# Hybrid mixer block on one core: projections with the hi and lo columns of x in one 512-column matmul per weight tile

## The chip, the cores and the metric

The kernel runs on one core of one Trainium2 chip. The metric is the device time of one execution in microseconds (us). The kernel before takes 1879.42 us, the median of three runs (1879.31 to 1880.51).

## The reference

One decoder layer on x of 256 tokens by 2048 channels, all in fp32. `w_in` projects the normalized input to the columns of three token mixers (RG-LRU, gated DeltaNet, RWKV-7) and of three merge gates; the mixers' outputs are projected, gated and summed, and a SwiGLU feed-forward part follows.

```python
h = rms_norm(x, norm_mix_pre)
p = h @ w_in                    # 2048 x 15664: columns of all mixers, then of the gates
lru_x, lru_g, qkv, z, beta_raw, alpha_raw, rw, gate_raw = split_cols(p, IN_SIZES)
y_a = rglru_branch(lru_x, lru_g, ...)
y_b = gated_deltanet_branch(qkv, z, beta_raw, alpha_raw, ...)
y_c = rwkv7_branch(rw, ...)
gates = sigmoid(gate_raw).reshape(B, S, 3, D)
mixed = sum_b gates[:, :, b] * (y_b @ w_branch[b])
x = x + rms_norm(mixed @ w_out, norm_mix_post)
x = x + rms_norm((silu(h2 @ w_gate) * (h2 @ w_up)) @ w_down, norm_ffn_post)   # h2 = rms_norm(x, norm_ffn_pre)
```

## The kernel before

Every large product is made from split operands. An fp32 value v is split into hi, v rounded to the format fp32r, and lo, v - hi; a product is then hi*hi + hi*lo + lo*hi, three fp32r matmuls that add up in the same PSUM bank. The input x is split once: `acts` (line 887) makes the tiles `xh` and `xl`, [128, 16, 256] each (16 k-tiles of 128 channels, 256 tokens), and `feed` (line 901) fills them, on ScalarE and on VectorE. The weights are split as they stream in: `weights` (line 190) loads 1 MB at a time into one of three `raw` tiles over SyncE's queue, ScalarE casts 1024 columns of it to `wh` (line 214), VectorE subtracts and gives `wl` (line 216), and there are three tiles of each.

Two helpers consume weights. `block_a` has tokens on the output partitions and streams 512 weight columns per matmul (lines 262 to 264); it makes the merge gates, the branch products, w_out and the feed-forward part. `block_b` (lines 228 to 246) has channels on the output partitions: the weight tile of 128x128 is the stationary operand and the 256 tokens are streamed, three matmuls for each k and each of two column tiles (lines 241 to 243), all into one PSUM bank [128, 2, 256]. It makes the mixers' projections: w_lo (256 columns), w_lo2 (128 columns) and 36 blocks of 256 columns of w_in. The tag `mm` of these banks has three buffers, which `block_a` uses too (two at a time).

When a bank is full, a sink empties it. `direct` (line 962) has VectorE multiply the bank with the tokens' norm factors `rbc` straight into a slab (`scaled`, line 339); `kept` (line 939, by `put_dram`, line 343) does the same into a stage tile, applies an activation on ScalarE and stores the tile in DRAM, from where `get` loads it later. The two lo blocks go by a ScalarE copy (`raw_slab`, line 948) and are scaled later, in SBUF.

The loop over q (lines 996 to 1011) runs four quarters; each has three rwkv blocks, three DeltaNet blocks and a kept z, and an LRU block and a kept gate, then the rest of the mixer chains, and some gate blocks (`fill`) as other work for TensorE. The mixers invert small triangular matrices (`inverse64`, line 369): 16x16 diagonal blocks go to DRAM and come back spread over all partitions (tile `B`, lines 381 to 384), 1 MB in an rwkv quarter and 512 KB in a DeltaNet pair. The branch products follow, then w_out, the norm, and the feed-forward part, which calls `acts` again for its own input; at the end the norm weights `n4` reuse the tag of `xl` and the output tile `od` that of `xh`.

The program's text sets dependencies and priorities, not the order. A planner simulates the engines in time and writes each engine's list from that; on the chip every engine works through its list in order.

Of the kernel before, what the change touches and what calls it, by code (L numbers as in the profile page):

```python
# [8 lines left out]
F32 = mybir.dt.float32  # L9
F32R = mybir.dt.float32r  # L10
# [4 lines left out]
P = 128  # L15
T = 256
# [62 lines left out]
def lay_out(inp):  # L79
# [43 lines left out]
    for g, key in enumerate(("lru_w_a", "lru_w_x")):  # L123
# [10 lines left out]
        "n2": f["norm_mix_post"], "n4": f["norm_ffn_post"], "w_in": blocks(w_in, 256), "w_mix": blocks(w[:, OFF_GATE:], 512),  # L134
# [6 lines left out]
class Builder:  # L141
# [86 lines left out]
    def block_b(self, wp, pp, src, xh, xl, kts, sink, width=256):  # L228

        for _ in self.block_b_steps(wp, pp, src, xh, xl, kts, sink, width):  # L230
            pass

    def block_b_steps(self, wp, pp, src, xh, xl, kts, sink, width=256):
        nc = self.nc
        ps = pp.tile([P, 2, 256], F32, name=self.uid("mm"), tag="mm", bufs=self.mm_bufs)
        nct = width // P
        for k, h, l in self.weights(wp, src, kts, width):
            for c in range(nct):
                hs, ls = h[:, c * P:(c + 1) * P], l[:, c * P:(c + 1) * P]
                o = ps[:, c]  # L240
                nc.tensor.matmul(o, hs, xh[:, k], start=(k == 0 and c == 0), stop=False, skip_group_check=True)  # L241
                nc.tensor.matmul(o, hs, xl[:, k], start=False, stop=False, skip_group_check=True)  # L242
                nc.tensor.matmul(o, ls, xh[:, k], start=False, stop=(k == kts - 1), skip_group_check=True)  # L243
            yield k
        with self.tc.high_priority(self.ahead_evac):
            sink(ps[:, :nct])
# [92 lines left out]
    def scaled(self, out, ps):  # L339

        self.nc.vector.tensor_tensor(out, ps, self.rbc.unsqueeze(1).to_broadcast([P, ps.shape[1], T]), ALU.mult)

    def put_dram(self, func):

        nc = self.nc
        d = self.dp.tile([P, 512], F32, name=self.uid("keep"))

        def sink(ps):
            t = self.sp.tile([P, 512], F32, name=self.uid("stage"), tag="stage", bufs=self.stage_bufs)
            self.scaled(t.rearrange("p (c t) -> p c t", c=2), ps)  # L350
            if func != AF.Copy:
                nc.scalar.activation(t, t, func)
            nc.scalar.dma_start(d, t)
        return sink, d
# [517 lines left out]
def build(tc, aps, out):  # L872
# [14 lines left out]
    def acts(s):  # L887
        return (xp.tile([P, KD, T], F32R, name=f"{s}h", tag="xh"), xp.tile([P, KD, T], F32R, name=f"{s}l", tag="xl"))
# [6 lines left out]
    xh, xl = acts("x")  # L895
# [40 lines left out]
    def cols(o, sink):  # L936
        b.block_b(wp, pp, w_in[o], xh, xl, KD, sink)

    def kept(o, func=AF.Copy):
        sink, d = b.put_dram(func)  # L940
        cols(o, sink)
        return d
# [5 lines left out]
    def raw_slab(t):  # L948
        return lambda ps: nc.scalar.copy(t[:, 0:ps.shape[1], 1:257], ps)

    b.block_b(wp, pp, aps["w_lo"][0], xh, xl, KD, raw_slab(lo))
# [3 lines left out]
    b.block_b(wp, pp, aps["w_lo2"][0], xh, xl, KD, raw_slab(lo2), width=128)  # L955
    b.scaled(lo[:, :, 1:257], lo[:, :, 1:257])
    b.scaled(lo2[:, 0:1, 1:257], lo2[:, 0:1, 1:257])
# [4 lines left out]
    def direct(o, lead):  # L962

        t = b.slab(lead)
        cols(o, lambda ps: b.scaled(t[:, :, lead:lead + T], ps))
        return t
# [10 lines left out]

    def stage(s):
        return sp.tile([P, 512], F32, name=b.uid(s), tag="stage", bufs=b.stage_bufs)
# [120 lines left out]
    xh, xl = acts("h")  # L1100
# [59 lines left out]
    n4 = full(xp, "n4", aps["n4"], tag="xl")  # L1160
    od = xp.tile([P, 2, D], F32, name="od", tag="xh")
# [38 lines left out]
```

## Time and profile before

| | before |
|---|---|
| median of 3 runs | 1879.42 us |
| profiled execution | 1879.03 us |
| its span, first to last instruction | 1877.3 us |
| TensorE matmuls busy | 1839.9 us, 98% |
| weight loads busy | 1591.6 us, 85% |
| VectorE busy | 1114.8 us, 59% |
| ScalarE busy | 850.5 us, 45% |
| mean granted TensorE clock | 0.988 of full speed |

Matmuls are pipelined: the profile lists each with a duration that overlaps the next one's, so their busy time adds up to a full engine, and what one costs in a row of them is the distance between starts. In the rows, PE is TensorE's matmuls, PEld its weight loads, DVE VectorE, ACT ScalarE, POOL GpSimd and SP SyncE; L241 is line 241; out<-in names the tiles. PEclk is the granted clock, 1.00 for 2.4 GHz. Some matmul records are missing from the trace; a row with x2 or more merges neighbours.

### The profile page before, as it was taken

Reading aid. Unit: us, or ns where it says so; the run is one execution under the profiler, and the core shown is the slowest. Engines: PE = TensorE matmul, PEld = TensorE weight load, DVE = VectorE, ACT = ScalarE, POOL = GpSimd, SP = SyncE. Lnnn points to the kernel's source line nnn. Section 1 sums busy time; section 2 is a strip of 40 time slices with the busy share of each in tenths; the row PEclk is TensorE's granted clock in tenths of the full one; section 3 lists DMA queues with packets and bytes.
Section 4 is the critical chain, followed back from the end, with each engine's and each line's share of the span. In section 5 each row is a group of like instructions: output and inputs, shape, how many; then the busy total and the mean of one; then the engine's idle time right before and its main releaser. Section 6 shows DMA issues by size and latency. Waiting matters only on the chain.

```text
span 1877.3 us, 27855 instructions
## 1 busy us (share of the span) xinstructions
PE 1839.9 (98%) x11516; PEld 1591.6 (85%) x11516; DVE 1114.8 (59%) x1622; ACT 850.5 (45%) x1055; POOL 82.6 (4%) x150
## 2 busy tenths in 40 slices
PE   9999999999999999899999999999999999999997
PEld 9999997999798988677888887888888888888886
DVE  6768667666776577656655556445545444444444
ACT  7445355434543465334444445444444444443442
POOL 0011010200120012000000000000000000000000
PEclk9999999999999999899999999999999999999999
DMA  7565445644565355648655556555555555555553
GB/s 263 183 183 200 141 152 189 169 162 153 178 168 175 134 183 174 202 164 310 209 194 183 195 186 234 194 196 184 194 187 191 191 181 199 204 200 188 194 200 114
DMA packets 61647, 352.06 MB, mean 188 GB/s; under 512 B 9040, under 2 KB 10832, under 8 KB 22480
## 3 DMA queue, kind: packets, MB, share of 16 engines
q1 hardware_dynamic: 50256, 327.18, 50.4%
q10 hardware_dynamic: 6752, 14.31, 2.1%
q0 software_dynamic: 4512, 8.79, 1.9%
q8 instruction: 90, 1.47, 0.3%
q14 instruction: 37, 0.30, 0.0%
HBM read 336.22 MB, written 14.02 MB: 187 GB/s over the span
## 4 chain that ended last, share of the span: by engine, by line
PE 53%; issue 38%; DMA 4%; DVE 3%; ACT 2%; POOL 1%; ACTq 0%; DVEq 0%; POOLq 0%; SPq 0%
PE mm L264 8%; PE mm L263 8%; PE mm L262 8%; PE mm L243 7%; PE mm L242 7%; PE mm L241 7%; DMA raw<-in_w_in_dram 2%; DVE wl L216 1%; DMA B<-dblk 1%; ACT wh L214 1%; PE psa L592 1%; PE pr L585 1%; PE pr L596 1%; PE px L562 0%; PE pst L602 0%
## 5 line engine op out<-in xcount | busy, mean ns | idle before, releaser
L216 DVE TENSOR_TENSOR wl<-raw,wh 128x1024 fp32r<-128x1024 f32 x590 | 720.9, 1223 | 616.8 <-ACT wh L214 614.6
L214 ACT CAST wh<-raw 128x1024 fp32r<-128x1024 f32 x590 | 620.1, 1052 | 856.9 <-PE mm L264 594.8
L241 PE MATMUL mm<-xh,wh 128*128 128x256 f32 x1200 | 344.4, 287 | 5.3 <-ACT wh L214 5.3
L243 PE MATMUL mm<-xh,wl 128*128 128x256 f32 x1200 | 344.9, 288 | 2.1 <-DVE wl L216 1.1
L242 PE MATMUL mm<-xl,wh 128*128 128x256 f32 x1200 | 345.0, 288 | 1.1 <-DVE xl L909 1.0
L263 PE MATMUL mm<-wl,hh 128*128 128x512 f32 x704 | 275.1, 391 | 0.5 <-DVE wl L216 0.5
L264 PE MATMUL mm<-wh,hl 128*128 128x512 f32 x704 | 274.8, 390 | 0.0
L262 PE MATMUL mm<-wh,hh 128*128 128x512 f32 x704 | 250.7, 392 | 2.0 <-DVE rstd L296 1.5
L241 PEld LDWEIGHTS mm<-xh,wh 128*128 128x128 f32 x1200 | 232.2, 194 | 7.5 <-ACT wh L214 6.0
L243 PEld LDWEIGHTS mm<-xh,wl 128*128 128x128 f32 x1200 | 231.9, 193 | 3.9 <-DVE wl L216 1.7
L242 PEld LDWEIGHTS mm<-xl,wh 128*128 128x128 f32 x1200 | 232.1, 193 | 2.4 <-DVE xl L909 1.5
L262 PEld LDWEIGHTS mm<-wh,hh 128*128 128x128 f32 x704 | 132.3, 188 | 29.4 <-ACT hh L311 2.5
L263 PEld LDWEIGHTS mm<-wl,hh 128*128 128x128 f32 x704 | 132.7, 189 | 27.8 <-DVE wl L216 0.7
L264 PEld LDWEIGHTS mm<-wh,hl 128*128 128x128 f32 x704 | 132.6, 188 | 27.5
L263 PE MATMUL mm<-wl,xh 128*128 128x512 f32 x384 | 151.0, 393 | 1.2 <-DVE wl L216 1.1
L264 PE MATMUL mm<-wh,xl 128*128 128x512 f32 x384 | 150.2, 391 | 0.0
L262 PE MATMUL mm<-wh,xh 128*128 128x512 f32 x384 | 139.5, 392 | 0.0
L263 PE MATMUL mm<-wl,ah 128*128 128x512 f32 x352 | 137.0, 389 | 0.0
L264 PE MATMUL mm<-wh,al 128*128 128x512 f32 x352 | 136.9, 389 | 0.0
L262 PE MATMUL mm<-wh,ah 128*128 128x512 f32 x352 | 123.5, 389 | 0.0
L297 POOL TENSOR_TENSOR rstd<-rstd,mhalf 128x8 f32<-128x8 f32 (+3 forms) x23 | 29.7, 1295 | 1453.7 <-DVE rstd L296 1453.7
L263 PEld LDWEIGHTS mm<-wl,xh 128*128 128x128 f32 x384 | 72.1, 188 | 17.8 <-DVE wl L216 2.5
(294 smaller groups left out, 2023.8 us busy)
## 6 DMA issues: line engine op xcount, KB each, us to landing
raw<-in_w_in_dram SPq DMA_DIRECT2D x72, 1024.0 KB, 4.9
raw<-in_w_mix_dram SPq DMA_DIRECT2D x48, 1024.0 KB, 4.9
raw<-in_w_gate_dram SPq DMA_DIRECT2D x44, 1024.0 KB, 4.9
raw<-in_w_up_dram SPq DMA_DIRECT2D x44, 1024.0 KB, 4.8
raw<-in_w_down_dram SPq DMA_DIRECT2D x44, 1024.0 KB, 4.9
raw<-in_w_branch_dram SPq DMA_DIRECT2D x24, 1024.0 KB, 4.9
raw<-in_w_out_dram SPq DMA_DIRECT2D x16, 1024.0 KB, 4.8
keep<-stage ACTq DMA_DIRECT2D x24, 256.0 KB, 5.2
```

The source lines that it names most:

```text
L214: nc.scalar.copy(wh[:, :n], s)
L216: nc.vector.tensor_tensor(wl[:, :n], s, wh[:, :n].bitcast(F32), ALU.subtract)
L241: nc.tensor.matmul(o, hs, xh[:, k], start=(k == 0 and c == 0), stop=False, skip_group_check=True)
L242: nc.tensor.matmul(o, hs, xl[:, k], start=False, stop=False, skip_group_check=True)
L243: nc.tensor.matmul(o, ls, xh[:, k], start=False, stop=(k == kts - 1), skip_group_check=True)
L262: nc.tensor.matmul(ps[t], xh[:, k, ts], h, start=(k == 0), stop=False)
L263: nc.tensor.matmul(ps[t], xh[:, k, ts], l, start=False, stop=False)
L264: return nc.tensor.matmul(ps[t], xl[:, k, ts], h, start=False, stop=(k == kts - 1))
L297: nc.gpsimd.tensor_tensor(r, r, self.mhalf.to_broadcast([P, n]), ALU.pow)
L585: nc.tensor.matmul(pq[bb, us], st[u][:, n, bb], sav[:, n, us], start=not n, stop=True, skip_group_check=True)
L592: nc.tensor.matmul(ps[bb, us], X[bb, 2 * u + p], R[bb, us], start=True, stop=True)
L596: nc.tensor.matmul(pq[ob, us], st[u][:, n, ob], sav[:, n, us], start=not n, stop=True, skip_group_check=True)
```

## The change

`w_in` is laid out in blocks of 128 columns in place of 256. xh and xl become the two halves of one tile x, [128, 16, 2, 256], so that for one k both stand side by side. `block_b` makes two matmuls for each k and column tile in place of three: hi of the weights with both halves of x as one moving operand of 512 columns, which fills a whole bank [128, 2, 256] (first half hi*hi, second half hi*lo), and lo of the weights with hi of x, 256 columns, added to the first half. Each column tile of 128 has a bank of its own. At the eviction `halves` has ScalarE copy the second half to SBUF and VectorE add the first; when both column tiles of a slab are there, `scaled` multiplies them in place. The stage tile of a kept block is taken before its matmuls. In the last part `n4` is loaded into a quarter of the output tile, since both halves of x are now one buffer.

```diff
-        "w_in": blocks(w_in, 256), "w_mix": blocks(w[:, OFF_GATE:], 512),
+        "w_in": blocks(w_in, P), "w_mix": blocks(w[:, OFF_GATE:], 512),
...
-    def block_b_steps(self, wp, pp, src, xh, xl, kts, sink, width=256):
+    def block_b(self, wp, pp, src, xs, kts, sink, width=P):
+
         nc = self.nc
-        ps = pp.tile([P, 2, 256], F32, name=self.uid("mm"), tag="mm", bufs=self.mm_bufs)
         nct = width // P
+        ps = [pp.tile([P, 2, 256], F32, name=self.uid("mm"), tag="mm", bufs=self.mm_bufs) for _ in range(nct)]
         for k, h, l in self.weights(wp, src, kts, width):
             for c in range(nct):
                 hs, ls = h[:, c * P:(c + 1) * P], l[:, c * P:(c + 1) * P]
-                o = ps[:, c]
-                nc.tensor.matmul(o, hs, xh[:, k], start=(k == 0 and c == 0), stop=False, skip_group_check=True)
-                nc.tensor.matmul(o, hs, xl[:, k], start=False, stop=False, skip_group_check=True)
-                nc.tensor.matmul(o, ls, xh[:, k], start=False, stop=(k == kts - 1), skip_group_check=True)
-            yield k
+                nc.tensor.matmul(ps[c], hs, xs[:, k], start=(k == 0), stop=False, skip_group_check=True)
+                nc.tensor.matmul(ps[c][:, 0], ls, xs[:, k, 0], start=False, stop=(k == kts - 1), skip_group_check=True)
         with self.tc.high_priority(self.ahead_evac):
-            sink(ps[:, :nct])
+            for c in range(nct):
+                sink(c, ps[c])
...
-    def scaled(self, out, ps):
-
-        self.nc.vector.tensor_tensor(out, ps, self.rbc.unsqueeze(1).to_broadcast([P, ps.shape[1], T]), ALU.mult)
...
+    def halves(self, out, ps):
+
+        self.nc.scalar.copy(out, ps[:, 1])
+        self.nc.vector.tensor_tensor(out, ps[:, 0], out, ALU.add)
+
+    def scaled(self, t):
+
+        self.nc.vector.tensor_tensor(t, t, self.rbc.unsqueeze(1).to_broadcast([P, t.shape[1], T]), ALU.mult)
...
     def acts(s):
-        return (xp.tile([P, KD, T], F32R, name=f"{s}h", tag="xh"), xp.tile([P, KD, T], F32R, name=f"{s}l", tag="xl"))
+        t = xp.tile([P, KD, 2, T], F32R, name=s, tag="x")
+        return t, t[:, :, 0], t[:, :, 1]
...
-    def cols(o, sink):
-        b.block_b(wp, pp, w_in[o], xh, xl, KD, sink)
-
-    def kept(o, func=AF.Copy):
-        sink, d = b.put_dram(func)
-        cols(o, sink)
+    def cols(o, t):
+
+        for c in range(2):
+            b.block_b(wp, pp, w_in[2 * o + c], xs, KD, lambda _, ps, c=c: b.halves(t[:, c], ps))
+        b.scaled(t)
+
+    def kept(o, func):
+
+        d = b.dp.tile([P, 512], F32, name=b.uid("keep"))
+        t = stage("stage")
+        cols(o, t.rearrange("p (c t) -> p c t", c=2))
+        nc.scalar.activation(t, t, func)
+        nc.scalar.dma_start(d, t)
         return d
...
-    def raw_slab(t):
-        return lambda ps: nc.scalar.copy(t[:, 0:ps.shape[1], 1:257], ps)
-
-    b.block_b(wp, pp, aps["w_lo"][0], xh, xl, KD, raw_slab(lo))
+    b.block_b(wp, pp, aps["w_lo"][0], xs, KD, lambda c, ps: b.halves(lo[:, c, 1:257], ps), width=256)
...
-        cols(o, lambda ps: b.scaled(t[:, :, lead:lead + T], ps))
+        cols(o, t[:, :, lead:lead + T])
...
-    n4 = full(xp, "n4", aps["n4"], tag="xl")
-    od = xp.tile([P, 2, D], F32, name="od", tag="xh")
+    od = xp.tile([P, 4, D], F32, name="od", tag="x")
+    n4 = od[:, 2]
+    nc.scalar.dma_start(n4, aps["n4"].to_broadcast([P, D]))
```

## Rows read from the trace of the kernel before

**Rows 1.** The page, part 1: busy us of each engine, share, instructions.
```profile
PE 1839.9 (98%) x11516; PEld 1591.6 (85%) x11516; DVE 1114.8 (59%) x1622; ACT 850.5 (45%) x1055; POOL 82.6 (4%) x150
```
**Rows 2.** Waits of TensorE: us in total, times, longest us.
```profile
PE mm L241 <- ACT wh L214: 5.3, 2, 3.0
```
**Rows 3.** Waits of VectorE for projection blocks: us in total, times, longest us.
```profile
DVE slab L341 <- PE mm L243: 11.7, 14, 1.6
DVE stage L341 <- PE mm L243: 5.6, 7, 1.2
```
**Rows 4.** Timeline, TensorE, projections: start us, duration us, instruction; first and last of 58.
```profile
53.09 0.28 PE L243 MATMUL mm<-xh,wl 128*128 128x256 f32 x1
...
59.93 0.28 PE L243 MATMUL mm<-xh,wl 128*128 128x256 f32 x1
```
**Rows 5.** Timeline, TensorE, w_down: first and last of 28.
```profile
1699.73 0.39 PE L263 MATMUL mm<-wl,ah 128*128 128x512 f32 x1
...
1705.85 0.39 PE L263 MATMUL mm<-wl,ah 128*128 128x512 f32 x1
```
**Rows 6.** Line 241: count, ns min/median/max, first and last start us.
```profile
L241 PE MATMUL mm<-xh,wh x1200: 277/283/580, 7.4 to 668.5; 128*128 128x256 f32 x172
```
**Rows 7.** Timeline, TensorE, two borders between a projection block and a gate block.
```profile
279.67 0.28 PE L243 MATMUL mm<-xh,wl 128*128 128x256 f32 x1
279.79 0.40 PE L262 MATMUL mm<-wh,xh 128*128 128x512 f32 x1
...
330.05 0.39 PE L264 MATMUL mm<-wh,xl 128*128 128x512 f32 x1
330.28 0.28 PE L241 MATMUL mm<-xh,wh 128*128 128x256 f32 x1
```
**Rows 8.** Timeline, TensorE, around 376 us; in brackets the idle time before.
```profile
376.06 0.39 PE L241 MATMUL mm<-xh,wh 128*128 128x256 f32 x1 [2.27 <-ACT wh L214]
...
377.31 0.58 PE L243 MATMUL mm<-xh,wl 128*128 128x256 f32 x1 [0.69 <-DVE wl L216]
...
378.12 0.41 PE L243 MATMUL mm<-xh,wl 128*128 128x256 f32 x1
...
381.96 0.42 PE L243 MATMUL mm<-xh,wl 128*128 128x256 f32 x1
```
**Rows 9.** Busy us by 25 us: PE, PEld, DVE, ACT, POOL; clock, DMA share, GB/s.
```profile
375.00:400.00 25.00, 23.26 (x295) 22.46 (x296) 20.19 (x66) 9.79 (x11) 0.00 (x0) 0.86 0.56 194
550.00:575.00 25.00, 21.53 (x167) 21.03 (x166) 15.90 (x37) 7.24 (x7) 0.00 (x0) 0.92 0.95 227
575.00:600.00 25.00, 24.02 (x401) 23.13 (x400) 19.19 (x64) 8.14 (x11) 0.00 (x0) 0.95 0.49 173
```
**Rows 10.** DMA issues: queue, count, KB each, median us from issue to landing.
```profile
raw<-in_w_in_dram SPq DMA_DIRECT2D x72, 1024.0 KB, 4.9
B<-dblk POOLq DMA_DIRECT2D x4, 1024.0 KB, 21.5
```
**Rows 11.** The chain of waits in order of time, 350 to 385 us: start us, us.
```profile
357.04 17.82 DMA raw<-in_w_in_dram
```
**Rows 12.** VectorE by line and shape: count, busy us, mean ns; idle before.
```profile
L341 DVE TENSOR_TENSOR slab<-mm,rbc 128x512 f32<-128x512 f32 x28 | 19.2, 686 | 11.7 <-PE mm L243 11.7
...
L859 DVE RECIPROCAL rec<-rec 128x512 f32<-128x512 f32 x4 | 13.4, 3350 | 0.1
...
L608 DVE TENSOR_TENSOR S<-S,pst 128x256 f32<-128x256 f32 x8 | 3.3, 417 | 9.7 <-PE pst L602 9.7
...
L341 DVE TENSOR_TENSOR slab<-slab,rbc 128x512 f32<-128x512 f32 x1 | 0.7, 693 | 0.5 <-ACT rbc L934 0.5
```
**Rows 13.** Line 949, the copies of the two lo blocks: ns min/median/max, first and last start us.
```profile
L949 ACT COPY slab<-mm x2: 367/466/564, 21.2 to 27.7; 128x512 f32<-128x512 f32 x1, 128x256 f32<-128x256 f32 x1
```
**Rows 14.** Busy us by 10 us, columns as in the 25 us stretches.
```profile
250.00:260.00 10.00, 10.00 (x89) 9.60 (x88) 10.00 (x23) 4.53 (x6) 1.30 (x2) 1.00 0.39 133
450.00:460.00 10.00, 10.00 (x90) 9.41 (x89) 10.00 (x24) 3.81 (x6) 0.11 (x1) 1.00 0.44 138
```

More of the change, by code (lines that the diff above doesn't have):

```diff
@@ L133, in lay_out @@
         "x": f["x"][0], "xt": f["x"][0].T.reshape(4, 4, P, T).transpose(0, 2, 1, 3), "par": par, "cst": constants(), "w_lo": blocks(lo[:, :256], 256), "w_lo2": blocks(lo[:, 256:], 128), "lru": lru, "up": up,
-        "n2": f["norm_mix_post"], "n4": f["norm_ffn_post"], "w_in": blocks(w_in, 256), "w_mix": blocks(w[:, OFF_GATE:], 512),
+        "n2": f["norm_mix_post"], "n4": f["norm_ffn_post"], "w_in": blocks(w_in, P), "w_mix": blocks(w[:, OFF_GATE:], 512),
         "w_branch": np.stack([blocks(f["w_branch"][0, i], 512) for i in range(3)]),
@@ L226, in warm_up @@
             self.nc.tensor.matmul(ps, self.rst128[:, 0:P], self.rst128[:, 0:P], start=True, stop=True)
-    def block_b(self, wp, pp, src, xh, xl, kts, sink, width=256):
-        for _ in self.block_b_steps(wp, pp, src, xh, xl, kts, sink, width):
-            pass
-    def block_b_steps(self, wp, pp, src, xh, xl, kts, sink, width=256):
+    def block_b(self, wp, pp, src, xs, kts, sink, width=P):
         nc = self.nc
-        ps = pp.tile([P, 2, 256], F32, name=self.uid("mm"), tag="mm", bufs=self.mm_bufs)
         nct = width // P
+        ps = [pp.tile([P, 2, 256], F32, name=self.uid("mm"), tag="mm", bufs=self.mm_bufs) for _ in range(nct)]
         for k, h, l in self.weights(wp, src, kts, width):
@@ L337, in slab @@
         return t
-    def scaled(self, out, ps):
-        self.nc.vector.tensor_tensor(out, ps, self.rbc.unsqueeze(1).to_broadcast([P, ps.shape[1], T]), ALU.mult)
[L343 to L354, printed above, removed]
+    def halves(self, out, ps):
[3 more added lines that the diff above has]
+        self.nc.vector.tensor_tensor(t, t, self.rbc.unsqueeze(1).to_broadcast([P, t.shape[1], T]), ALU.mult)
     def get(self, d, s):
@@ L892, in build @@
     mp = b.mp = b.pool("mp")
-    xh, xl = acts("x")
+    xs, xh, xl = acts("x")
     xt = [b.u4("x") for _ in range(4)]
@@ L934, in by_token, with stage @@
         nc.scalar.copy(b.rbc, ps[:, 0:T])
-    def cols(o, sink):
-        b.block_b(wp, pp, w_in[o], xh, xl, KD, sink)
-    def kept(o, func=AF.Copy):
-        sink, d = b.put_dram(func)
-        cols(o, sink)
+    def stage(s):
+        return sp.tile([P, 512], F32, name=b.uid(s), tag="stage", bufs=b.stage_bufs)
+    def cols(o, t):
[8 more added lines that the diff above has]
+        nc.scalar.dma_start(d, t)
         return d
@@ L954, in build @@
     input_rms()
-    b.block_b(wp, pp, aps["w_lo2"][0], xh, xl, KD, raw_slab(lo2), width=128)
-    b.scaled(lo[:, :, 1:257], lo[:, :, 1:257])
-    b.scaled(lo2[:, 0:1, 1:257], lo2[:, 0:1, 1:257])
+    b.block_b(wp, pp, aps["w_lo2"][0], xs, KD, lambda c, ps: b.halves(lo2[:, c, 1:257], ps))
+    b.scaled(lo[:, :, 1:257])
+    b.scaled(lo2[:, 0:1, 1:257])
     b.rwkv_lo(lo, lo2)
@@ L976, in gate_block @@
         b.block_a(wp, pp, aps["w_mix"][j], xh, xl, KD, sink)
-    def stage(s):
-        return sp.tile([P, 512], F32, name=b.uid(s), tag="stage", bufs=b.stage_bufs)
     def fill(n):
@@ L1099, in build @@
     x1d = [b.dp.tile([P, D], F32, name=f"x1d{t}") for t in range(2)]
-    xh, xl = acts("h")
+    _, xh, xl = acts("h")
     with tc.high_priority(FIRST):
```

## The prediction

> **What bounds the kernel now.** I read the busy shares first [rows 1]: TensorE's matmuls fill 1839.9 of 1877.3 us. A busy TensorE is not yet a TensorE at its peak, so its list of waits came next [rows 2]: the longest entry is 5.3 us for cast weights, and no eviction of a projection block stands in it. VectorE's own list shows the opposite: for 14 + 7 of the 36 evictions it was VectorE that waited for the matmuls, at most 1.6 us [rows 3]. So in nearly the whole span the time is the sum of what is queued on TensorE. What a matmul costs there is not its listed duration (0.28 us, pipelined), but the distance of starts. In a long row of 256-column matmuls the first and the last of 58 stand at 53.09 and 59.93 us [rows 4]: 6.84/57 = 0.1200 us. In a row of 512-column ones 28 stand between 1699.73 and 1705.85 us [rows 5]: 6.12/27 = 0.2267 us. The difference, 106.7 ns for 256 columns, is the 2.4 GHz level; both leave the same remainder, 120.0 - 106.7 = 13.3 ns and 226.7 - 213.3 = 13.4 ns, whatever the width. At full clock a matmul thus costs its columns plus 13.3 ns.
>
> **The change part by part.** *Fewer, wider matmuls.* A group is one weight tile of 128x128 at one k; there are 1200 of them [rows 6]: 36 blocks of w_in with 2 x 16, w_lo with 32, w_lo2 with 16. Before, a group is three matmuls of 256 columns, 3 x 120.0 = 360.0 ns. After, it is one of 512 and one of 256, 226.7 + 120.0 = 346.7 ns. The columns are the same 768; what goes is one remainder of 13.3 ns and one weight load. 1200 x 13.3 ns = 16.0 us. That needs the two widths to keep their distances when they alternate, which the trace shows only at borders between blocks: a 512 right after a 256 starts 0.12 us behind it, and a 256 right after a 512 0.23 us behind [rows 7], each the distance that belongs to the earlier one's width. I take both as they are, since these rows are the nearest; the bounds are all of the 16.0 us and none.
>
> The Trainium skill (TensorE: Matmul & The Clock Gate, section "Wait — 56ns, not 53.3ns?") gives a fixed cost of about 2.5 ns for a warm matmul, which speaks against the change: an estimate by it is 1200 x 2.5 ns = 3.0 us of gain in place of 16.0. The two distances above show 13.3 ns for this kernel's fp32r matmuls, so the trace does not agree, and the measurement decides.
>
> *Where the saving is lost again.* (a) Half clock. After TensorE had stood still for 2.27 and 0.69 us, starts from 378.12 to 381.96 us lie 3.84/18 = 0.213 us apart for 256 columns [rows 8], which is the 1.2 GHz level; the remainder is gone there, and a group of 768 columns costs 640 ns either way. The granted clock of the stretches around the two stops, 0.86 of 25 us and then 0.92 and 0.95 of 25 us [rows 9], makes 7.0 and 4.0 + 2.5 us at half: 13.5/0.64 = 21 groups without a gain, 0.3 us. (b) Two waits for weights. These stops stand behind the 1 MB transfer that spreads the diagonal blocks (median 21.5 us to landing, against 4.9 for a w_in load [rows 10]); in the chain of waits one w_in load beside it takes 17.82 us [rows 11]. TensorE lives on loaded weights then, for about 22 us or 22/0.36 = 61 groups; it uses them up 61 x 13.3 ns = 0.8 us sooner and waits for the same transfer. Twice, 1.6 us. (c) The start. The first matmuls wait for x; half of w_lo's 32 groups, as I estimate, are fed by arrivals, 16 x 13.3 ns = 0.2 us. That the first matmul of a k now needs lo as well as hi of x costs nothing more, since its successor waited for lo before too.
>
> *Evictions.* Before, 36 blocks each took one multiply of 128x512 on VectorE (0.69 us [rows 12]), the two lo blocks a ScalarE copy each (0.564 and 0.367 us [rows 13]). After, each of 75 column tiles takes a ScalarE copy of 128x256 out of PSUM (0.367 us, the shorter lo copy) and a VectorE add of 128x256 with one operand in PSUM (0.417 us, as the state add [rows 12]); the multiplies stay, now from SBUF (0.693 us, as the one on the first lo slab [rows 12]). Added: on ScalarE 75 x 0.367 - 0.93 = 26.6 us, on VectorE 75 x 0.417 = 31.3 us. The bounds for the time are nothing and all of it, 57.9 us; below nothing it can't go, as it takes no more than the 0.93 us off any engine. I take nothing, because no eviction holds TensorE now and VectorE is busy for 59%, ScalarE for 45% of the span [rows 1]. What covers it are the PSUM banks: three, so a bank must be free two blocks after it is full. That cover was 2 x 96 x 0.120 = 23.0 us and becomes 2 x 16 x 0.3467 = 11.1 us, against 0.37 + 0.42 us of work plus the queues. Behind the copy on ScalarE stand the casts of the next weights and the activations of the mixers; behind the add on VectorE the lo halves of those weights. A finished slab comes 0.37 + 0.42 = 0.8 us later; its readers are mixer chains that TensorE meets between other blocks. If that cover fails, the price is rival 2.
>
> *Edits at nothing.* w_in as blocks of 128 columns still comes in 72 loads of 1 MB, 8 KB per partition, and a 1024-wide cast holds eight groups where it held four pairs, so transfers and casts keep their number; if a load took longer, more waits as in (b) would pay for it. One tile for both halves of x is as large as the two were, and its next user is the norm ahead of the feed-forward part, behind all three branch products. The norm weights for the end now lie in the output tile; their load waits for the same last matmuls as before, and has the first w_down block (44 x 2 x 3 matmuls of 0.2267 us, 60 us) in which to arrive. Taking the stage tile ahead of the matmuls can hold back a gate block for one projection block at most, and TensorE has the projection itself to do meanwhile.
>
> *The sum.* 16.0 - 0.3 - 1.6 - 0.2 = 13.9 us. The profiled execution took 1879.03 us (its span of 1877.3 and 1.7 around it), 0.39 under the median of the three runs, 1879.42. 1879.03 - 13.9 = 1865.1; from the median 1865.5. I say 1865.3 us.
>
> **The rivals.** (1) *A stop more or less.* The order on each engine comes from a planner that simulates time, so changed durations can change the order around the big transfers. A stop as the one at 374 us costs 2.27 + 0.69 us of standing still and 7.0/2 = 3.5 us for the half clock, 6.5 us. One fewer, with the rest of the sum: 1865.1 - 6.5 = 1858.6; one more: 1871.6. For it: that transfer runs in all four quarters and makes a stop in projections in two of them, so it hangs on little. Against: neither the transfer nor its place in the program is touched.
> (2) *Slower, by the bank cover.* VectorE was busy for all of 10 us in stretches where projections run, at 250 and at 450 us [rows 14]. An eviction that crosses two in-order queues and has 11.1 us of cover instead of 23.0 could hold a bank there, TensorE would stop, and the clock fall as in (a). At 6.5 us a stop the sum turns at 13.9/6.5 = 2.1 stops; one in each of three quarters gives 1865.1 + 19.5 = 1884.6. For it: that the same stretch recurs. Against: TensorE did not wait there once (10.00 us busy), and the longest single VectorE instruction, the reciprocal, takes 3.35 us [rows 12].
> (3) *The change doesn't do what it says.* If the 13.3 ns did not belong to each matmul, so that a 512 and a 256 in turn took 360 ns, nothing would be saved: 1879.0. Against it stand the two borders [rows 7]; for it, that they are only two. The skill's 2.5 ns would put the time at an estimated 1876.0, between this case and the forecast.
>
> **How the numbers follow.** The forecast (1861 to 1869) gets 0.66, one stop fewer 0.08, one more but still faster 0.08, no change (rival 3, or two further stops that eat the gain) 0.08, slower by the banks 0.10. A measurement of this kernel can tell about 0.2%, 3.8 us, from no change. That gives 0.82 faster, 0.08 same, 0.10 slower. The range takes in the forecast and both sides of rival 1: from all 16.0 us and one stop fewer, 1879.03 - 16.0 - 6.5 = 1856.5, to one stop more with another 2 us lost, 1873.6; I give 1857 to 1874, with 0.18 left out.
>
> **What would show it.** In the profile after, the two new lines have 1200 matmuls of 512 and 1200 of 256 columns, in turn 0.227 and 0.120 us apart, and TensorE has 10316 matmuls in place of 11516. The last projection group, which began at 668.5 us [rows 6], should begin near 655, and all that follows should keep its length. TensorE's list of waits should not name the add or the copy; if it does, or if stretches of half clock appear beside those near 375 and 570 us, rival 2 is at work. Pairs that take 0.36 us would be rival 3. A shift in the second half, where only the tiles' places change, would make the working wrong.

## The result: 0.95% slower

The changed kernel takes 1897.93 us (median of four runs, 1892.13 to 1900.62) against 1879.37 us for the kernel before on the same chip: a ratio of 1.0095, 95% interval 1.0069 to 1.012. The forecast was 1865.3 us, its range 1857 to 1874. The profiled execution has a span of 1890.4 us, 13.1 more than the 1877.3 of before. It is the fastest of its four, so its trace shows 13.1 of the 18.6 us between the medians; the other three have no trace, and their granted clock was 0.981 to 0.982 in place of 0.986.

The page of after, part 1 (busy us, share, instructions; before: [rows 1]):

```profile
PE 1830.2 (97%) x10316; PEld 1522.0 (81%) x10316; DVE 1137.4 (60%) x1697; ACT 873.6 (46%) x1129; POOL 84.9 (4%) x150
```

TensorE has its 1200 matmuls fewer and is busy for 9.8 us less (1830.17 against 1839.95 to two decimals). It stands still for the rest of the span, 60.2 us where before has 37.3, 22.9 us more: -9.8 + 22.9 = +13.1. That is the whole difference between the two profiled executions, and what has to be explained is the standing still.

Where it lies, by stretches of before (first fence) and after (second); columns: stretch, its us, then busy us of PE, PEld, DVE, ACT, POOL, clock, DMA share, GB/s. The last stretch begins with w_out in both.

```profile
50.00:725.00 675.00, 667.60 (x5759) 616.70 (x5758) 470.39 (x880) 318.49 (x417) 60.10 (x101) 0.99 0.53 170
725.00:850.00 125.00, 116.92 (x892) 94.64 (x891) 78.63 (x165) 52.14 (x76) 12.22 (x20) 0.92 0.56 180
1037.60:1877.30 839.70, 822.52 (x3680) 680.80 (x3678) 423.12 (x418) 362.48 (x423) 7.94 (x10) 0.99 0.54 191
```

```profile
50.00:725.00 675.00, 653.59 (x4624) 547.71 (x4623) 483.80 (x941) 336.36 (x483) 58.74 (x100) 0.99 0.53 169
725.00:850.00 125.00, 107.98 (x866) 88.94 (x865) 80.60 (x171) 54.09 (x79) 14.91 (x23) 0.90 0.51 161
1050.70:1890.40 839.70, 822.51 (x3680) 680.54 (x3678) 423.27 (x418) 362.53 (x423) 8.98 (x10) 0.99 0.55 191
```

The second half keeps its length to the tenth. In the projections TensorE stands still for 675 - 653.6 = 21.4 us (before 7.4), between 725 and 850 us for 17.0 (before 8.1). The last projection group begins at 665.6 us, 2.9 us earlier than before [rows 6] and not the 13 of the forecast. The waits of TensorE in after (us in total, times, longest us; before: [rows 2]) name the engine:

```profile
PE px L396 <- DVE DT L392: 14.5, 1, 14.5
PE mm L237 <- DVE wl L216: 6.6, 4, 3.8
PE mm L236 <- DVE stage L336: 3.5, 1, 3.5
PE mm L236 <- ACT wh L214: 2.8, 2, 1.6
PE mm L256 <- DVE stage L336: 2.3, 2, 1.2
```

L336 is the new add: 3.5 + 2.3 us are matmuls that wait for a PSUM bank. The larger sums are older work on VectorE, the lo halves of weights (L216) and a step of the last quarter's chain (L392). The added instructions are as long as estimated, 0.416 and 0.368 us (columns as in [rows 12]):

```profile
L336 DVE TENSOR_TENSOR slab<-mm,slab 128x256 f32<-128x256 f32 x59 | 24.2, 416 | 0.0
L335 ACT COPY slab<-mm 128x256 f32<-128x256 f32 x59 | 21.3, 368 | 7.2 <-DVE cv L641 6.9 <-PE mm L237 0.3
```

How an add comes to hold TensorE shows in the timeline of after around 267 us (start us, us, engine):

```profile
263.77 0.37 ACT L335 COPY stage<-mm 128x256 f32<-128x256 f32 x1
264.47 0.42 DVE L594 TENSOR_TENSOR S<-S,pst 128x256 f32<-128x256 f32 x1
264.80 0.48 DVE L641 SCALAR_TENSOR_TENSOR cv<-slab,par_t,cv 128x256 f32<-128x256 f32 x1
265.20 1.22 DVE L216 TENSOR_TENSOR wl<-raw,wh 128x1024 fp32r<-128x1024 f32 x1
266.33 0.48 DVE L641 SCALAR_TENSOR_TENSOR cv<-slab,par_t,cv 128x256 f32<-128x256 f32 x1
266.73 0.42 DVE L336 TENSOR_TENSOR stage<-mm,stage 128x256 f32<-128x256 f32 x1
...
267.20 0.80 PE L236 MATMUL mm<-x,wh 128*128 128x512 f32 x1 [3.47 <-DVE stage L336]
```

The copy is done at 264.14, but four instructions stand before the add in VectorE's queue; the add starts at 266.73, 2.6 us later, and TensorE gets the bank at 267.20. In before, TensorE did not stop in this stretch. The 25 us stretches of after, answering to [rows 9] and [rows 14]:

```profile
250.00:275.00 25.00, 21.53 (x141) 18.61 (x140) 18.95 (x42) 11.04 (x19) 1.52 (x4) 0.93 0.27 96
375.00:400.00 25.00, 21.73 (x114) 18.31 (x113) 16.47 (x46) 8.95 (x12) 0.00 (x0) 0.93 0.85 211
450.00:475.00 25.00, 20.60 (x136) 17.20 (x135) 17.74 (x41) 10.50 (x18) 2.10 (x3) 1.00 0.30 102
575.00:600.00 25.00, 19.58 (x102) 16.48 (x102) 14.97 (x43) 7.73 (x10) 0.00 (x0) 0.93 0.84 202
```

Last, the pace. The timeline of after has these two rows of pairs, 512 and 256 columns in turn. In the first there are fifteen 512-column starts from its first line to its last, in the second 58:

```profile
54.71 0.40 PE L236 MATMUL mm<-x,wh 128*128 128x512 f32 x1
54.94 0.28 PE L237 MATMUL mm<-x,wl 128*128 128x256 f32 x1
...
59.65 0.40 PE L236 MATMUL mm<-x,wh 128*128 128x512 f32 x1
...
178.35 0.40 PE L236 MATMUL mm<-x,wh 128*128 128x512 f32 x1
...
198.11 0.39 PE L236 MATMUL mm<-x,wh 128*128 128x512 f32 x1
```

4.94/14 = 0.3529 us a pair in the first and 19.76/57 = 0.3467 in the second; only the second has the pace of the forecast. Over the 1069 pairs of the trace that follow each other directly, 0.33 to 0.37 us apart, the mean is 0.3503 (the expectations of e3 and e8 below say 0.3526, which the trace does not bear out); the 1057 triples of before, counted alike, have 0.3594. That is a saving of 9.1 ns a group, 10.9 us for all 1200 at full clock, close to the 9.8 us by which TensorE's busy time fell.

### The profile page after: what moved, and what is told of

Its sections match the earlier page's. It is cut to its first block, busy times and chain, and to the rows that moved or that the text cites. A ratio compares the mean times of both kernels' runs of the same rounds, so it can differ in the third digit from the quotient of the medians.

```text
span 1890.4 us, 25603 instructions
## 1 busy us (share of the span) xinstructions
PE 1830.2 (97%) x10316; PEld 1522.0 (81%) x10316; DVE 1137.4 (60%) x1697; ACT 873.6 (46%) x1129; POOL 84.9 (4%) x150
## 4 chain that ended last, share of the span: by engine, by line
issue 38%; PE 27%; DMA 2%; DVE 2%; ACT 1%; POOL 0%; DVEq 0%; POOLq 0%; ACTq 0%
PE mm L257 7%; PE mm L258 7%; PE mm L256 7%; PE mm L236 2%; DMA B<-dblk 1%; PE mm L237 1%; DMA raw<-in_w_branch_dram 1%; DVE wl L216 0%; DVE x L1101 0%; PE psa L578 0%; PE pr L571 0%; PE pr L582 0%; PE pst L588 0%; DVE xt L378 0%; PE tp L279 0%
## 5 line engine op out<-in xcount | busy, mean ns | idle before, releaser
L216 DVE TENSOR_TENSOR wl<-raw,wh 128x1024 fp32r<-128x1024 f32 x590 | 720.4, 1223 | 629.8 <-ACT wh L214 628.5
L236 PE MATMUL mm<-x,wh 128*128 128x512 f32 x1200 | 432.0, 402 | 8.0 <-DVE stage L336 3.5
L237 PE MATMUL mm<-x,wl 128*128 128x256 f32 x1200 | 342.9, 286 | 6.7 <-DVE wl L216 6.6
L236 PEld LDWEIGHTS mm<-x,wh 128*128 128x128 f32 x1200 | 227.8, 190 | 61.7 <-DVE stage L336 3.7
L257 PE MATMUL mm<-wl,h 128*128 128x512 f32 x704 | 274.8, 390 | 0.5 <-DVE wl L216 0.5
L258 PE MATMUL mm<-wh,h 128*128 128x512 f32 x704 | 274.8, 390 | 0.0
L256 PE MATMUL mm<-wh,h 128*128 128x512 f32 x704 | 250.8, 391 | 2.0 <-DVE rstd L290 1.5
L237 PEld LDWEIGHTS mm<-x,wl 128*128 128x128 f32 x1200 | 229.4, 191 | 9.9 <-DVE wl L216 8.4
L256 PEld LDWEIGHTS mm<-wh,h 128*128 128x128 f32 x704 | 132.3, 188 | 29.5 <-ACT h L305 2.5
L258 PEld LDWEIGHTS mm<-wh,h 128*128 128x128 f32 x704 | 132.6, 188 | 27.6
L257 PE MATMUL mm<-wl,x 128*128 128x512 f32 x384 | 151.5, 395 | 0.0
L258 PE MATMUL mm<-wh,x 128*128 128x512 f32 x384 | 150.6, 393 | 0.0
L256 PE MATMUL mm<-wh,x 128*128 128x512 f32 x384 | 142.7, 395 | 2.3 <-DVE stage L336 2.3
L256 PEld LDWEIGHTS mm<-wh,x 128*128 128x128 f32 x384 | 72.3, 189 | 18.5 <-DVE stage L336 2.7
L258 PEld LDWEIGHTS mm<-wh,x 128*128 128x128 f32 x384 | 72.5, 189 | 15.3 <-issue 0.7
```

What stands on the lines that cost most here:

```text
L216: nc.vector.tensor_tensor(wl[:, :n], s, wh[:, :n].bitcast(F32), ALU.subtract)
L236: nc.tensor.matmul(ps[c], hs, xs[:, k], start=(k == 0), stop=False, skip_group_check=True)
L237: nc.tensor.matmul(ps[c][:, 0], ls, xs[:, k, 0], start=False, stop=(k == kts - 1), skip_group_check=True)
L256: nc.tensor.matmul(ps[t], xh[:, k, ts], h, start=(k == 0), stop=False)
L257: nc.tensor.matmul(ps[t], xh[:, k, ts], l, start=False, stop=False)
L258: return nc.tensor.matmul(ps[t], xl[:, k, ts], h, start=False, stop=(k == kts - 1))
```

## The experiments

Two theories stood against each other. *Work*: the added copies and adds take time on VectorE and ScalarE that the mixers' chains need. *Order*: the planner, given other durations, puts the instructions of VectorE in another sequence, and TensorE waits behind it. Diffs are against the kernel named in bold; "ratio" is to the kernel before. The first three kernels below (e1 to e3) were planned anew, so each holds another order besides its edit.

### Which part of the change costs

**After**, each column tile evicted by one multiply of the first half (the three lo tiles by one ScalarE copy), and without the multiply of the whole slab:

```
-        self.nc.scalar.copy(out, ps[:, 1])
-        self.nc.vector.tensor_tensor(out, ps[:, 0], out, ALU.add)
...
+            self.nc.vector.tensor_tensor(out, ps[:, 0], self.rbc, ALU.mult)
```

> The changed kernel, but each column tile is emptied by one instruction: VectorE multiplies the first half of the bank by the norm factors straight into its place (the three lo tiles: one ScalarE copy). The second half of the bank, hi of the weights by lo of x, is left out of the result; the matmuls that make it are all there. Theory A (the added ScalarE copies and VectorE adds slow the mixers' chains, and the chains set the time, so the saving on TensorE is lost): without them the saving is kept, 1879 less 5 to 9 us, 1868 to 1876 us. Theory B (the evictions are covered; the planner's other order and the late weight loads cost the time): it stays near the changed kernel, 1890 to 1900 us.

1883.56 us, ratio 1.002 (1.0005 to 1.0035): about 14 us of the loss is gone with the evictions, but no gain appears. That lies between the two expectations.

**Before** with the change's evictions (a ScalarE copy times 0 and a VectorE add for each column tile, the multiply then from SBUF):

```
+            self.nc.scalar.mul(out[:, c], ps[:, c], 0.0)
+            self.nc.vector.tensor_tensor(out[:, c], ps[:, c], out[:, c], ALU.add)
```

> The kernel before, its matmuls untouched, but each 128x256 column tile is emptied as in the change: a ScalarE instruction out of PSUM (here times zero, so that the sum stays right), a VectorE add with the bank, and the 128x512 multiply in SBUF afterwards. Theory A: slower than before by 10 to 25 us, 1889 to 1904 us, with the quarter's chain steps later than in the kernel before by 10 us or more at the last of the rwkv chains. Theory B: within 4 us of before, 1875 to 1883 us.

1896.53 us, ratio 1.0093 (1.0076 to 1.0111). The evictions alone, with the order that the planner gives them, make a loss as large as the whole change's.

**After** with three matmuls of 256 columns:

```
-                nc.tensor.matmul(ps[c], hs, xs[:, k], start=(k == 0), stop=False, skip_group_check=True)
+                nc.tensor.matmul(ps[c][:, 0], hs, xs[:, k, 0], start=(k == 0), stop=False, skip_group_check=True)
+                nc.tensor.matmul(ps[c][:, 1], hs, xs[:, k, 1], start=False, stop=(k == kts - 1), skip_group_check=True)
```

> The changed kernel with only the merging undone: three matmuls of 256 columns per weight tile again (hi*hi into the first half of the bank, hi*lo into the second, lo*hi into the first), everything else as in the change. Theory A: TensorE's matmuls are not what sets the time there, so about the time of the changed kernel, 1892 to 1902 us. Theory C (the shorter groups are worth their 7.4 ns each, 0.3526 against 0.3600 us, and the rest of the change costs a fixed amount): 1200 x 7.4 ns = 9 us above the changed kernel, 1905 to 1909 us.

1899.35 us, ratio 1.0113 (1.0093 to 1.0132). Inside the change the merge is worth 3.4 us by the two ratios, whose intervals overlap. In the profiled executions TensorE is busy for 1851.7 us here and stands still for 46.8; after has 1830.2 and 60.2. Of these 21.5 us of busy time only some 11 can be the merge's (10.9 by the paces above); the granted clock was 0.981 here and 0.986 in after. So the two executions don't show how much of the merge's saving comes back as standing still.

### What a pair costs

A kernel of matmul streams only, with nothing of the mixer: 96 groups a stage, some with VectorE and ScalarE kept busy beside them.

> Only TensorE's streams, on resident operands, the rest of the layer left out: 96 pairs of a 512- and a 256-column matmul in a row, four times after different short interruptions, then with VectorE, with ScalarE and with both at work beside them; 96 triples of 256 columns alone and beside both; 192 matmuls of 512. What the changed kernel shows is 0.3526 us a pair on the mean, with stretches at 0.3467 and at 0.3533. If the alternation itself costs a step, every stretch shows 0.3533; if traffic of the other engines does, only the last ones do and the first show 0.3467; if it hangs on how a row of matmuls begins, the four interruptions differ. Triples 0.360 and 512 alone 0.2267 in any case.

First and last of 46 starts of the first matmul of a pair, in a stage with idle engines and in one with VectorE and ScalarE busy (the windows show how busy); then 41 starts of triples, both engines busy:

```profile
49.67 0.40 PE L888 MATMUL ps<-xs,wh 128*128 128x512 f32 x1
65.57 0.40 PE L888 MATMUL ps<-xs,wh 128*128 128x512 f32 x1
...
229.94 0.40 PE L888 MATMUL ps<-xs,wh 128*128 128x512 f32 x1
245.54 0.39 PE L888 MATMUL ps<-xs,wh 128*128 128x512 f32 x1
...
300.07 0.28 PE L893 MATMUL ps<-xs,wh 128*128 128x256 f32 x1
314.47 0.28 PE L893 MATMUL ps<-xs,wh 128*128 128x256 f32 x1
```

```profile
50.00:66.00 16.00, 16.00 (x93) 13.88 (x92) 0.00 (x0) 0.00 (x0) 0.00 (x0) 1.00 0.00 0
230.00:246.00 16.00, 16.00 (x94) 13.99 (x94) 15.55 (x14) 15.53 (x16) 0.00 (x0) 1.00 0.00 1
```

15.90/45 = 0.3533 and 15.60/45 = 0.3467 us a pair; 14.40/40 = 0.3600 a triple. Once it runs, a stage keeps one of the two paces to its end: two of the seven stages of pairs ran at 0.3533, five at 0.3467, and busy neighbours are not what decides: the two slow stages had idle engines beside them, and all three with VectorE or ScalarE busy ran at 0.3467. So a group saves 6.7 or 13.3 ns. What sets the pace is open; the number of fp32 matmuls ahead of a stage, which I varied for it, doesn't do it alone (after four of them both paces occurred).

### How much the order alone does

**Before**, and **after**, with one more gate block held back for the end (AHEAD 9 in place of 8): no work is added.

```
-AHEAD = 8
+AHEAD = 9
```

> The changed kernel with one more gate block made ahead of the branch products (9 in place of 8), so that TensorE has 96 matmuls, 22 us, more to do in the tail of the last quarter; the sum of the work is the same. Theory A: the 14.5 us for which TensorE stands at 781 us, waiting for the last chain, are filled, and with the clock that stays up the time falls by 14 to 20 us, to 1876 to 1884 us. Theory B (that stop is made by a late load of branch weights that queue ahead of the chain on VectorE, and moves with it): it stays, 1890 to 1900 us.

> The kernel before with one more gate block made ahead (9 in place of 8), the same edit that took about 10 us off the changed kernel. Theory A (the end is set by the last quarter's chains in the kernel before too; its TensorE stands 3.9 us and then runs some 20 us at half clock around 780 us): 5 to 12 us less, 1867 to 1874 us. Theory D (before, TensorE's own work sets the end, and only the change made the chains the bound): within 4 us of before, 1875 to 1883 us.

After becomes 1887.84 us, ratio 1.0053 (1.0034 to 1.0072); before becomes 1866.42 us, ratio 0.9941 (0.9926 to 0.9956). The first lies between its two expectations, the second just beyond the 5 to 12 us of theory A. In before's own profile TensorE's stop of 3.9 us at 780 us comes with a low granted clock (0.59 on the mean from 775 to 800 us, the row near the end of this part); with AHEAD 9 both are gone:

```profile
775.00:800.00 25.00, 24.67 (x333) 19.60 (x332) 16.49 (x45) 11.34 (x15) 0.00 (x0) 1.00 0.60 210
```

Of the 12.1 us by which this profiled execution is shorter, 4.5 are less standing still and 7.6 less busy time for the same matmuls: the mean granted clock is 0.994 in place of 0.988.

**Before** with 72 unused instructions at the evictions, 128x256 each: copies on ScalarE (e6), adds on VectorE (e7).

```
+        for c in range(ps.shape[1]):
+            self.nc.scalar.copy(self.rst128, ps[:, c])                                             # e6
+            self.nc.vector.tensor_tensor(self.rst128, ps[:, c], self.rst64[:, 0:T], ALU.add)       # e7
```

> The kernel before with 72 extra ScalarE copies of 128x256 out of the projection banks into an unused tile, one for each column tile of w_in, ahead of the multiply; nothing waits for their result but the bank. They take ScalarE's time (72 x 0.37 = 27 us) without lengthening what a chain waits for. Theory A1 (the cost is the place the added instructions take in the engines' lists): 4 to 12 us slower than before, 1883 to 1891 us. Theory A2 (the cost is the longer way from the last matmul to the finished slab, 0.8 us and two queues per block): within 3 us of before, 1876 to 1882 us.

> The kernel before with 72 extra VectorE adds of 128x256 out of the projection banks into an unused tile (72 x 0.42 = 30 us), nothing waits for their result but the bank. VectorE is the busier of the two (59% against 45%, and full around each chain), so by theory A1 most of the changed kernel's loss shows here: 8 to 18 us slower than before, 1887 to 1897 us. Theory A2: within 3 us of before, 1876 to 1882 us.

The copies, 26.6 us of useless work, make the kernel *faster*: 1864.97 us, ratio 0.9933 (0.9916 to 0.9949). The adds, 30.0 us, give 1886.20 us, ratio 1.0041 (1.0026 to 1.0057). For e6 neither theory expected that, and e7 falls just short of what A1 expected. Work can't make a kernel faster, so both were repeated with the finished order of every engine kept, instruction for instruction, and the unused instructions shortened to 16 columns. This edit comes behind the planner:

```
+            blk.instructions[at] = make(kind, dict(kw, ins=tuple(cut(p) for p in i.ins), outs=tuple(cut(p) for p in i.outs)))
```

> e7_vector_only with its order kept instruction for instruction and the 72 unused additions on VectorE cut from 256 to 16 columns, so that the order stands and the work is gone; nothing that the output needs is left out. If e7_vector_only lost by its order, it stays within 3 us of 1886.2; if by the 30.0 us of VectorE work in the way of the chains, it is within 3 us of 1878.5 or under it.

> e6_scalar_only with its order kept instruction for instruction and the 72 unused copies on ScalarE cut from 256 to 16 columns; nothing that the output needs is left out. If e6_scalar_only won by its order, it stays at 1865.0 or a few us under it; if by anything that the copies' work does, it goes back towards 1878.5.

e12 takes 1883.92 us, ratio 1.0028 (1.0017 to 1.0039); e13 takes 1865.28 us, ratio 0.9927 (0.9912 to 0.9942). Both do the work of before plus 72 instructions of 0.17 us (12 us in all, on VectorE in e12 and on ScalarE in e13) whose results nobody uses; for the rest they differ in order, and lie 18.6 us apart. More than half of e7's loss is left in e12: that part is its order's, but for what the short adds cost. e6's gain is all order. TensorE's longest wait in e12, and its busy time in e13 from 50 to 725 us (only 0.7 us idle):

```profile
PE px L417 <- DVE DT L413: 15.8, 1, 15.8
```

```profile
50.00:725.00 675.00, 674.32 (x5846) 623.49 (x5846) 478.12 (x898) 332.69 (x495) 65.64 (x107) 1.00 0.53 173
```

### What the work does, with the order held

In the same way: **after** with its 75 adds cut to 16 columns (e9), and **before** with the second matmul of each group cut to 224 columns (e11), which was meant to take off TensorE just the 16.0 us that I had given to the merge.

```
+    shorter(nc, "Builder.halves", 16, lambda i: "DVE" in str(i.engine))                                                      # e9
+    shorter(nc, "Builder.block_b_steps", 224, lambda i: type(i).__name__ == "InstMatmult" and i.ins[0].memref.startswith("xl_"))  # e11
```

> The kernel after with the order of every engine kept as it is, instruction for instruction, and only the 75 additions on VectorE (L336) cut from 256 to 16 columns; 240 columns of each first half are left out. It takes some 20 to 25 us off VectorE (75 x 416 ns before the cut) and leaves the order, the waits and the 75 copies on ScalarE. If the work of the additions holds the chains up, the second st product of the last quarter comes at 745 or earlier (after: 760; before: 739) and the time is 1884 or less. If the order in which the planner put the steps sets it, that product stays at 755 or later and the time within 4 us of 1898.

> The kernel before, its order kept instruction for instruction, with one thing changed: the second matmul of each of the 1200 groups of three (L242, weights of hi with lo of x) streams 224 columns and not 256; 32 columns of that term are left out. 32 columns at 2.4 GHz are 13.3 ns, so TensorE gets just the 16.0 us that the forecast gave to the merge, with the eviction and the order untouched. If the matmuls' queue on TensorE is the time, 14 to 16 us are gained (1863 to 1865). If the last quarter's chain through VectorE, ScalarE and DMA sets the end, less than 8 us are gained (1871 or more), though the last group of the projections ends 14 us earlier.

e9: 1888.52 us, ratio 1.0047 (1.0032 to 1.0062). The adds' work is thus worth some 9 of 18 us, give or take 6 by the two intervals; the last st product comes at 754 us, between the two expectations.

e11: 1871.23 us, ratio 0.9953 (0.9939 to 0.9968). The narrower matmul took less off TensorE than meant. Ten starts of the first matmul of a group, first and last:

```profile
647.86 0.28 PE L241 MATMUL mm<-xh,wh 128*128 128x256 f32 x1
...
651.01 0.28 PE L241 MATMUL mm<-xh,wh 128*128 128x256 f32 x1
```

3.15/9 = 0.3500 us a group. Over 1059 groups, counted as above, the mean is 0.3496 against 0.3594 in before: 9.8 ns, 11.7 us in all and not 16.0. Of these, 7.2 us arrive by the medians; the five executions reach from 1866.9 to 1871.3, 11.5 to 7.1 us under the median of before. In the profiled one, the fastest, the span is 12.1 us shorter and TensorE stands still for 38.4 us against 37.3 before: there, with the order held, the whole saving arrived, and the chain moved with TensorE (its last st product comes at 729.1 in place of 739.6 us). So in before TensorE's queue is most of what sets the time; where some 4 us go in the slower executions no trace shows.

### What the places in VectorE's queue do

The waits of after point at single instructions. **After** with all its work and one, then six, of VectorE's 1697 instructions elsewhere in its queue; then the six moves with the adds cut as in e9:

```
+    move(nc, [(1056, 216, 1098)])                                                                                               # e14
+    move(nc, [(361, 336, 357), (519, 216, 511), (639, 336, 637), (793, 216, 785), (926, 336, 924), (1056, 216, 1098)])         # e15
```

> The kernel after with one of VectorE's 1697 instructions elsewhere in its queue, all work kept: the lo half of the w_branch weights (L216) at which VectorE stood idle for 6.13 us until 788.48 us, waiting for a load, with the finished inputs of the last quarter's chain (xt, xc) queued behind it, goes behind that chain (after DT L392). If the place in VectorE's in-order queue makes TensorE's wait of 14.5 us for DT, that wait falls to about 8 us and the kernel gains 5 to 7 us on after (1891 to 1893). If the added work alone makes the loss, or if another wait takes the place, it stays within 2 us of 1897.9.

> As e14_one_moved, with five more moves, all work kept: two lo halves of w_in weights (the ones of 393.88 and 593.77 us) ahead of the chain step that waited 7 us for the B load, and three of the additions out of PSUM (266.73, 468.73, 669.24 us) ahead of the convolution steps and the lo half that stood before them. If the planner's places cost the time, the waits of 3.5, 2.3 and most of the 6.6 us go as well, with part of the half clock behind them: 1878 to 1886. If the added work sets it, nothing more is gained than in e14_one_moved, or the stops come back elsewhere: 1890 or more.

> e15_six_moved with the 75 additions cut to 16 columns as in e9_short_adds (240 columns of each first half are left out). If work and places are two separate causes, the 9 us that the cut gave in the order of after come on top of what the moves give: 1869 to 1877. If they are one (the additions are late because of what stands before them), the two together give little more than the larger of them, 1880 or more.

e14: 1894.83 us, ratio 1.009 (1.0075 to 1.0105), no clear gain. The wait that was taken away hid another one: in e14 VectorE waits for the B load instead, and TensorE still stands for 11.6 us.

```profile
787.86 0.28 DVE L378 TENSOR_TENSOR xt<-B,xc 128x120 f32<-128x120 f32 x1 [4.24 <-DMA B<-dblk]
```

```profile
793.56 0.65 PE L396 MATMUL px<-DT,U 32*32 32x32 f32 x32 [11.60 <-DVE DT L392]
```

e15: 1889.03 us, ratio 1.0057 (1.0037 to 1.0078), 7 us under after by the two ratios, whose intervals just overlap, and less than the 12 or more that I expected. The waits for banks (L336) fall from 5.8 to 1.2 us, and TensorE stands still for 53.3 us instead of 60.2. e16: 1884.51 us, ratio 1.0035 (1.0018 to 1.0053). Cut and moves give some 9 and 7 us alone, and 11 together. That points to largely one cause, adds that come late because of what stands before them; but each of these figures is uncertain by some 6 us, so that two causes that add up to 16 are not ruled out.

### The last quarter's chain

In all kernels the span ends 1123 to 1139 us after the last quarter's second st product begins (the last start of the line that is L562 in before and L548 in after). The ratio is that of the medians, the other columns are of the profiled execution:

| kernel | ratio | span us | TensorE busy | still | last st at | span - st |
|---|---|---|---|---|---|---|
| before | 1 | 1877.3 | 1839.9 | 37.3 | 739.6 | 1137.7 |
| after | 1.0095 | 1890.4 | 1830.2 | 60.2 | 761.1 | 1129.3 |
| e1 one op | 1.0020 | 1881.5 | 1829.2 | 52.3 | 747.5 | 1134.0 |
| e2 before + evictions | 1.0093 | 1895.7 | 1843.8 | 51.9 | 764.1 | 1131.6 |
| e3 three matmuls | 1.0113 | 1898.5 | 1851.7 | 46.8 | 761.3 | 1137.2 |
| e4 after, AHEAD 9 | 1.0053 | 1889.6 | 1837.1 | 52.5 | 766.2 | 1123.4 |
| e5 before, AHEAD 9 | 0.9941 | 1865.2 | 1832.4 | 32.8 | 738.1 | 1127.1 |
| e6 copies | 0.9933 | 1863.0 | 1834.3 | 28.7 | 725.1 | 1137.9 |
| e7 adds | 1.0041 | 1884.8 | 1839.2 | 45.6 | 752.0 | 1132.8 |
| e9 after, adds cut | 1.0047 | 1883.4 | 1828.5 | 54.9 | 754.2 | 1129.2 |
| e11 before, 224 columns | 0.9953 | 1865.2 | 1826.8 | 38.4 | 729.1 | 1136.1 |
| e12 order of e7 | 1.0028 | 1883.4 | 1836.8 | 46.6 | 751.4 | 1132.0 |
| e13 order of e6 | 0.9927 | 1864.4 | 1834.5 | 29.9 | 725.2 | 1139.2 |
| e14 one moved | 1.0090 | 1890.5 | 1831.9 | 58.6 | 761.7 | 1128.8 |
| e15 six moved | 1.0057 | 1886.1 | 1832.8 | 53.3 | 758.7 | 1127.4 |
| e16 moved, adds cut | 1.0035 | 1882.8 | 1831.5 | 51.3 | 753.6 | 1129.2 |

The last st moves over 41 us and the rest over 16. The two kernels with AHEAD 9 have the shortest rests, 1123.4 and 1127.1: more work for TensorE beside the chain helps there. What may keep the rest nearly fixed is in the chain of waits of *before* from 740 us on (start us, us):

```profile
740.88 1.21 DVE st L564 x2
742.38 3.08 POOL dblk L381 x6
...
746.02 1.73 DMA dblk<-st
...
748.41 19.70 DMA B<-dblk
...
768.87 1.06 ACT wh L214
```

After st come the diagonal blocks, a 1 MB load that takes 19.7 us, and then steps of xt and xc on VectorE; TensorE has gate blocks for some of this time and then nothing else. In the stretch from 775 us it was busy for 19.08 us in before (first fence) and for 10.35 in after (second):

```profile
775.00:800.00 25.00, 19.08 (x381) 16.13 (x380) 13.75 (x53) 8.07 (x19) 0.00 (x0) 0.59 0.38 136
```

```profile
775.00:800.00 25.00, 10.35 (x169) 7.90 (x169) 17.79 (x76) 6.76 (x7) 0.00 (x0) 0.73 0.76 211
```

TensorE's stop in before, 3.9 us at 780 us, is for ScalarE's cast of a branch input (L1032) behind these steps; in after it is the 14.5 us for the chain's DT (L392). In after this chain starts 21.5 us later. That the merge also brings TensorE to the wait with less left to do is argued and not shown.

What stays open: e16 is still 0.35% over before, and some 17 us over what before would take with the merge's 10.9 us off. Part of it is order that six moves don't reach, part may be the copies on ScalarE, which lie in each eviction's path. Shortening the copies alone in after's order was not tried. And since e1 and e2 hold orders of their own, and orders alone lie 18.6 us apart, their 14 and 18 us are not shown to be the evictions' work; with the order held only the 9 us of e9 are.

## Why the prediction was wrong

*"In nearly the whole span the time is the sum of what is queued on TensorE."* As a sum this holds (busy plus still is the span), and the matmul count, the unchanged second half, the number of loads and casts and the lengths of the added instructions came out as worked out. But the 37.3 us of standing still were taken for a constant, and they became 60.2. Where no instruction was added and no place in a queue changed, they did stay, in the one execution with a trace (e11: 38.4), so what failed is not the sum but the two steps that were to keep the other term still: evictions at nothing, and an order taken for fixed. Some of the 37.3 us, 8.1 from 725 to 850 us, lie in the last quarter's chain. The rows for it were in the profile: the chain of waits runs through st and the B load, and TensorE is busy for only 19.08 of 25 us at 775. The text used the B load only as a neighbour that delays w_in loads [rows 10, 11].

*Evictions at nothing.* This is the step that failed. The reason given was that no eviction held TensorE and that VectorE was busy for 59% [rows 1]. Neither says what stands before an instruction in an in-order queue at the moment it becomes ready. In before an eviction was a single VectorE instruction; in after it crosses two queues, and at 267 us it waits 2.6 us in the second. The term was costed at 0 with an upper bound of 57.9; the evictions with the order drawn for them cost 18 us on before's own matmuls (e2), a third of the way up, and with the order held the adds alone some 9 (e9).

*Rival 2, banks.* Its mechanism occurs: three waits for L336, 3.5 us at 267 and 2.3 us at 469 and 670, as many as the rival had counted, the first two some 10 us behind the stretches that [rows 14] had pointed at and the clock down with the first (0.93). It was given 0.10 because VectorE's longest instruction is 3.35 us against a cover of 11.1; what counts is the sum of the queue, not its longest member. And it is the smaller part: 5.8 us, of 22.9 more than before.

*Rival 1, the planner's order.* One stop more or less was priced at 6.5 us, "for it: that it hangs on little". With the work all but equal two orders lie 18.6 us apart (e12, e13), nearly three times that price, and a changed duration can draw a new one. The range should have reached that far on both sides.

*The merge's 16.0 us.* The term was mis-sized by the reading of [rows 7]: distances of 0.12 and 0.23 us with two decimals can't tell 0.3467 from 0.3533 a pair, and the borders are single events. Measured are 9.1 ns a group, 10.9 us, since the pairs of after run at either pace. Rival 3, no saving, was wrong as well. By the fixed cost of 2.5 ns a warm matmul in the Trainium skill (TensorE: Matmul & The Clock Gate, section "Wait — 56ns, not 53.3ns?") it would have been an estimated 3.0 us; the 10.9 us measured here lie between that and the 16.0 of the forecast.

*The losses (a) to (c)*, 2.1 us in all, had the right places (375 and 575 us) but took the order for fixed.

## What to carry to other kernels

When the busiest engine is busy for 98%, ask what it does in the other 2%, and what could make that grow: here it went from 37.3 to 60.2 us while the busy time fell by 9.8. A stop can cost more than its length: in e5, where before's stop at 780 us is gone and the clock stays up there, the busy time is 7.6 us shorter too. An added instruction on an engine that is half idle costs what stands ahead of it in that engine's queue, so it is priced at the place where it is queued, from the timeline, and not by the engine's share. Where a planner sets the order, first measure how far the time moves when only the order changes (here 18.6 us, more than the gain in question); a better order can be worth more than the edit: before with AHEAD 9 is 0.59% faster, and before with 72 tiny unused copies 0.73%.

## What the hardware showed that I had not expected

A stream of fp32r matmuls of 512 and 256 columns in turn has two steady paces, 0.3533 and 0.3467 us a pair, and keeps the one it starts with; the three stages with VectorE or ScalarE busy beside them (up to 97% of the time) all ran at 0.3467. Triples of 256 columns keep 0.3600 us in both stages of them that were run. Narrowing the middle one of three from 256 to 224 columns, all else kept, gave 9.8 ns a group (0.3594 to 0.3496 us), not the 13.3 ns that 32 columns are at the 106.7 ns for 256 of [rows 4, 5].
